# Entry of the SSD stage in a fused attention, SSD and conv-FFN layer: a quarter of the second output row ahead of the first row's second half, z tiles and weight splits in written order, GpSimd's z products and ScalarE's clamps later

## The chip, the core and the metric

The kernel runs on one core of a Trainium2 chip. TensorE (PE) multiplies matrices out of SBUF into PSUM, which has eight banks. VectorE (DVE), ScalarE (ACT) and GpSimd (POOL) work on tiles of 128 partitions; SyncE (SP) issues most DMAs. Each engine takes its own instructions strictly in order and waits at semaphores for the others. The metric is the device time of one execution in microseconds (us), smaller is better. Before the change it is 1199.05 us, the median of 3 runs from 1198.35 to 1201.15.

## What is computed

One layer on 1024 rows of 1024 columns: a norm with modulation, one input projection, attention beside a Mamba-2 scan (SSD), the output projection with a gated residual, a second norm and a convolutional feed-forward net. The change lies in the SSD part and in the output projection:

```python
z, xbc, dt_raw, q, k, v = jnp.split(h @ w_in[l], IN_SPLITS, axis=-1)
...
y = ssd_scan(xs * dt[..., None], dt * A, bm, cm)
y = y + d_skip.astype(jnp.float32)[:, None] * xs
y = y.reshape(b, s, SSD_WIDTH) * jax.nn.silu(z.astype(jnp.float32))
return rmsnorm(y, norm_w).astype(z.dtype)
...
x = x + g_m * (jnp.concatenate([y_ssd, y_att], axis=-1) @ w_out[l])
```

## The kernel before

Every large product is made of three matmuls: each operand is split into a high part, which ScalarE rounds, and a low part, which VectorE gets by subtraction, and TensorE adds high by high, high by low and low by high (`split`, line 84, and `mm3`, line 79). So each operand of a product costs one ScalarE and one VectorE instruction before TensorE may use it.

The 1024 rows are worked in 8 blocks of 128 rows (NT = 8). In the order of the program:

1. The norm, the projection and the attention (to about 300 us) fill `ya`, the attention half of the mixer's output, block by block.
2. The convolved columns fill `xs`, `bt_` and `ct_`. Then come **z tiles** (`z_tile`, line 765): 8 tiles of one half of the z columns (`ch` 1, with dt), then 8 tiles of the other half (`ch` 0), each 24 matmuls into a PSUM tile named `zps` or `s`, a Tanh or Silu on ScalarE and a product on VectorE into `zs`. Behind the first tile of `ch` 0 stands `dt_prep`, which makes the decays (`sm`, `ex3`, `acc_`) for all chunks, and `ssd_pre` for chunk 0.
3. During the same tiles the output projection's weights are split (`wout_split`, line 731) into the room that the z tiles' left operand gives up: slots 0 to 3 (`hH0`, `hL0`), the weights of the attention part, and behind chunk 0 the slots 4 to 7 (`hH1`, `hL1`), those of the SSD part, in 8 pieces of 512 columns scaled by the norm's weight.
4. **The SSD loop** (from line 1061) goes over chunks c = 0 to 7 of 128 rows. `ssd_y` multiplies the masked decay matrices with the inputs (`ydp`, 8 small matmuls), the state with C (`yop`) and B with the inputs (`stp`), and adds them up on VectorE. `ssd_norm` multiplies by z and normalizes: VectorE, ScalarE's Square, two GpSimd instructions for the inverse root (`rstd`), ScalarE's scale. `ssd_turn` transposes the result into `xs`. `ssd_pre` prepares the next chunk: `xdt` on VectorE, `xdd` on GpSimd, 8 clamps (Relu) of the decay rows `cr` on ScalarE, four matmuls into `xps`, `cb` on VectorE, two Exp on ScalarE into `th` and two products of `th` and `cb` on VectorE, which `ydp` of the next chunk needs.
5. Between these, `wout_half(n)` fills TensorE: 24 matmuls of the output projection for block n // 2, the attention part for even n, the SSD part for odd n. They go to two PSUM banks (`wops`), one for each half of the output columns, and the two parts of a block add up in them. The left operand is `yhl`, split from `ya` or `xs` by `wout_rhs`; the odd halves need `xs` after `ssd_turn`. `wout_row` then adds the residual and takes the second norm.

Before the change chunk c goes with half n = c. The halves 8 to 15 follow in the next stage, between the transposes of the second norm (`h_raw`).

The Tile framework places instructions by a scheduler, not always as written: within an engine the order is free as far as data allow, unless `tc.issue_after(i)` puts an instruction behind `i` on the same engine, or `InOrder` (line 49) is switched on. The SSD loop's matmuls are chained in written order by `pe`; the z tiles' are not. GpSimd's product of the finished z with the decay (`zs` times `sm["t"]`, line 867) stands at the end of `ssd_pre` and is free to go early: 6 of the 8 stand ahead of all other GpSimd work of the stage.

Of the kernel before, what the change touches and what calls it, by code (L numbers as in the profile page):

```python
# [68 lines left out]
def tile_block(ctx: ExitStack, tc: tile.TileContext, x, ccol, pk, w_ada, w_first, w_ft, w_z,  # L69
# [41 lines left out]
    def stat(n=1):  # L111
# [3 lines left out]
        stc[0] += n  # L115
        return a

    def rstd(ms, eps=EPS):
        n = ms.shape[-1]
        r = stat(n)  # L120
        G.tensor_scalar(ms, ms, eps, 1.0, op0=ALU.add, op1=ALU.mult)
        G.tensor_tensor(r, ms, mhalf[:, 0:n], ALU.pow)
        return r

    nc.sync.dma_start(cc, ccol)
# [605 lines left out]
    def wout_split(slot, t):  # L731
        dh, j = WORDER[slot]
        h, l = (n[slot // 4][:, slot % 4].rearrange("p a b -> p (a b)") for n in (hth, htl))
        with tc.issue_after(pin[0]), tc.issue_after(pin[1]):
            if j < 2:
                split(h, l, t, A, V)
            else:
                for b in range(2):
                    c = slice(512 * b, 512 * b + 512)
                    k = SNW + order[2 * j + b]  # L740
                    split(h[:, c], l[:, c], t[:, c], A, V, scale=pkt[:, k:k + 1])
# [23 lines left out]
    def z_tile(ch, st, wz):  # L765
        if st < 2 or st // 2 == (3, 2)[ch]:
            ps = psv.tile([P, 512], F32, tag=("acc", "pv")[st % 2], bufs=1, name="zps")[:, 0:260]
        else:
            ps = s_tile()[:, 0:260]
        for kt in range(KT):  # L770
            mm3(ps, hth[st // 4][:, st % 4, kt, :], htl[st // 4][:, st % 4, kt, :],
                wz[kt // 2][0][:, kt % 2, :],
                wz[kt // 2][1][:, kt % 2, :], kt == 0, kt == KT - 1)
        if ch == 1:
            A.activation(zs[:, st, 260:512], ps[:, 0:252], AF.Silu)
            V.tensor_tensor(zs[:, st, 512:520], ps[:, 252:260], pkt[:, DTB:DTB + 8], ALU.add)
            return
        z = zs[:, st, 0:260]
        A.activation(z, ps[:, 0:260], AF.Tanh)
        zlast[:] = [V.scalar_tensor_tensor(z, z, 1.0, ps[:, 0:260], op0=ALU.add, op1=ALU.mult).ins]  # L780

    def dt_prep():
        dtr = zs[:, :, 512:520]
# [45 lines left out]
    def pe(op, *a, **k):  # L829
        with tc.issue_after(chain[0]) if chain and chain[0] else ExitStack():  # L830
            i = op(*a, **k)  # L831
        if chain:
            chain[0] = i.ins

    def ssd_pre(c, xp_, between=None):
# [3 lines left out]
        V.tensor_tensor(h8(xdt), h8(xs[:, c, :]), hb("dt", c), ALU.mult)  # L839
        G.tensor_tensor(h8(xdd), h8(xdt), hb("de", c), ALU.mult)  # L840
        ms_ = []
        cr = bcp.tile([P, 8, P], F32, tag="rm", bufs=2, name="cr")
        nc.sync.dma_start(cr, rows_from(acd, 8 * c, 8))
        for g in range(2):
            for k in range(4 * g, 4 * g + 4):
                a = acc_[:, 8 * c + k:8 * c + k + 1]
                A.activation(cr[:, k], cr[:, k], AF.Relu, scale=-1.0, bias=a)
# [15 lines left out]
            pin2 = V.tensor_tensor(m, m, cb[:, g:g + 1, :].to_broadcast([P, 4, P]), ALU.mult)  # L863
            ms_.append(m)
        pin[:] = [pin1.ins, pin2.ins]
        with tc.issue_after(pin1.ins):
            G.tensor_tensor(h8(zs[:, c, 0:512]), h8(zs[:, c, 0:512]), hb("t", c), ALU.mult)
        return xdt, xdd, cb, ms_

    wz = wz_weights(1)  # L870
# [22 lines left out]
    wz = wz_weights(0)  # L893
    wout_get(3, 6)
    for st in range(NT):
        z_tile(0, st, wz)
        if st == 0:
            dt_prep()
            pin0 = list(pin)
            pre0 = ssd_pre(0, tp_tile)  # L900
            pin[:] = pin0
# [21 lines left out]
        return ps2b.tile([P, 512], F32, tag="x", bufs=PB[1], name="xps")  # L923

    def ssd_tile(name):
        return ps2a.tile([P, 512], F32, tag="ssd", bufs=PB[3], name=name)

    def ssd_y(c, xdt, xdd, cb, ms_):
        cs = slice(c * P, (c + 1) * P)
# [13 lines left out]
        if c < NT - 1:  # L943
            stp = ssd_tile("stp")
            for g in range(2):
                pe(T.matmul, stp[:, g * 256:g * 256 + 256], cb[:, 2 + g, :],
                   xdd[:, g * 256:g * 256 + 256], start=True, stop=True)
            if c > 0:
                G.tensor_tensor(h8(cur), h8(prev), hb("cd", c), ALU.mult)
# [6 lines left out]
            V.tensor_tensor(y, y, t, ALU.add)  # L956
        return y, t

    gated = []

    def ssd_norm(c, y, t, at=None):
        with tc.issue_after(at) if at else ExitStack():
            gated[:] = [V.tensor_tensor(y, y, zs[:, c, 0:512], ALU.mult).ins]
        ms = stat()
        A.activation(t, y, AF.Square, accum_out=ms)
        r = rstd(ms, 512.0 * EPS)
        A.activation(y, y, AF.Copy, scale=r)

    def ssd_turn(c, y):
        tps = x_tile()  # L970
        for j in range(4):
            pe(T.transpose, tps[:, j * P:(j + 1) * P], y[:, j * P:(j + 1) * P], ident)
        A.activation(xs[:, c, :], tps, AF.Copy)


    x1d = dram.tile([S, D], F32, name="x1d")
# [21 lines left out]
    def wout_half(n, ks=slice(0, 8), fill=()):  # L998
        st, part = n // 2, n % 2
        if ks.start == 0:  # L1000
            if part == 0:
                if not xrs:
                    xrs.append(wu.tile([P, 2, 2, 512], F32, tag="w2", bufs=1, name="xr"))
                xr_[st] = xrs[0][:, st % 2]
                nc.sync.dma_start(xr_[st].rearrange("p a b -> p (a b)"), x[st * P:(st + 1) * P, :])
                wps[st] = [ps2b.tile([P, 512], F32, tag="wo", bufs=PB[0], name="wops")
                           for _ in range(2)]
            for q in ((0,), (2,))[n] if n < 2 else (n + 1,):
# [52 lines left out]
    for c in range(NT):  # L1061
# [4 lines left out]
            ssd_turn(*turn)  # L1066
        if c == 1:
            at = wout_rhs(0, 1)
        if c > 1:
            ssd_norm(c, y, t)  # L1070
        turn = (c, y)
        if c < NT - 1:
            pre = ssd_pre(c + 1, x_tile, lambda: wout_half(c, slice(0, 3)))
            if c < 2:
                ssd_norm(c, y, t, at)
            row_scale(pin[0])
            wout_half(c, slice(3, 8))
            if c == 0:
                for j in range(4, 8):
                    pin[:] = zlast + gated  # L1080
                    wout_split(j, wt[j])
        else:
            wout_half(c)
    ssd_turn(*turn)
    chain[:] = []
    row_scale()
# [605 lines left out]
```

## Time and profile before

| quantity | value |
|---|---|
| median of 3 runs | 1199.05 us |
| the profiled execution, whole | 1199.13 us |
| its span, first to last instruction | 1197.4 us |
| TensorE busy | 1166.5 us (97%), mean granted clock 0.990 |
| VectorE, ScalarE, GpSimd busy | 909.2, 588.5, 157.4 us |
| last z tile's last matmul ends | 408.77 us |
| first `ydp` of the SSD loop starts | 413.56 us |
| `ydp` of chunk 2 starts | 439.23 us |
| end of the 16 output halves | about 549.2 us |

A row of the timeline reads: start, duration, engine, line, operation, output<-inputs, size, and in brackets how long the engine was idle before it and what released it. A row with xN merges N instructions in a row. In a table of stretches, each engine has its busy time and number of instructions; PEclk is the clock granted to TensorE as a share of full speed. Engine busy times do not say which wait ends last; the waits and the chain of work do.

### The profile page before, as it was taken

To read this page: it belongs to the slowest core of one execution; us is meant where nothing else is said; L and a number is where in the kernel's file an instruction comes from. 1 tells how busy PE (TensorE), PEld (TensorE's weight loads), DVE (VectorE), ACT (ScalarE), POOL (GpSimd) and SP (SyncE) were. 2 spreads that over 40 slices of the span, in tenths; PEclk is the share of its full clock that TensorE was granted. 3 is DMA by queue.
4 is the path that set the end of the run, shared out by engine and by line. 5 is a ranking of instruction groups with operands and counts; after the bars stand their busy time and mean duration, and the time that the engine had idled before them with its cause. 6 is when DMAs were issued, how large, how long until landed. Compare 5 with 4: busy or idle time off the path is not lost.

```text
span 1197.4 us, 15744 instructions
## 1 busy us (share of the span) xinstructions
PE 1166.5 (97%) x5839; PEld 979.5 (82%) x5839; DVE 909.2 (76%) x1357; ACT 588.5 (49%) x970; POOL 157.4 (13%) x178
## 2 busy tenths in 40 slices
PE   8999999899999899999999999999999999999996
PEld 7778888788789888888788888888888888888885
DVE  7736556665795788558999988898888869666986
ACT  5626555564234766577543453344433444433454
POOL 1103343330000545100000000000000000000522
PEclk9999999899999899999999999999999999999998
DMA  9736334201585322240233222332233378633444
GB/s 355 257 91 158 100 125 115 69 1 36 212 273 184 109 86 72 76 145 28 90 130 129 82 88 97 132 109 85 97 106 114 114 260 301 248 116 122 158 133 148
DMA packets 61293, 160.24 MB, mean 134 GB/s; under 512 B 6608, under 2 KB 7072, under 8 KB 59808
## 3 DMA queue, kind: packets, MB, share of 16 engines
q1 hardware_dynamic: 53872, 134.19, 34.1%
q10 hardware_dynamic: 7344, 25.04, 5.3%
q8 instruction: 46, 0.75, 0.3%
q14 instruction: 31, 0.25, 0.1%
HBM read 121.15 MB, written 28.61 MB: 125 GB/s over the span
## 4 chain that ended last, share of the span: by engine, by line
PE 82%; DVE 10%; issue 3%; ACT 2%; DMA 1%; POOL 1%; POOLq 0%; DVEq 0%; ACTq 0%; SPq 0%
PE wops L831 6%; PE dn L82 5%; PE dn L80 5%; PE dn L81 5%; PE uY L80 5%; PE uY L82 5%; PE uY L81 5%; PE uX L82 3%; PE uX L80 3%; PE uZ L81 3%; PE uZ L80 3%; PE uX L81 3%; PE uZ L82 3%; PE s L80 2%; PE s L81 2%
## 5 line engine op out<-in xcount | busy, mean ns | idle before, releaser
L81 PE MATMUL dn<-w 128*128 128x512 f32 x296 | 108.1, 391 | 0.0
L80 PE MATMUL dn<-w 128*128 128x512 f32 x296 | 108.1, 391 | 0.0
L82 PE MATMUL dn<-w 128*128 128x512 f32 x296 | 100.2, 391 | 0.2 <-DVE w L90 0.2
L80 PE MATMUL uY<-tH,w 128*128 128x512 f32 x248 | 97.2, 392 | 0.0
L81 PE MATMUL uY<-tL,w 128*128 128x512 f32 x248 | 97.0, 391 | 0.0
L82 PE MATMUL uY<-tH,w 128*128 128x512 f32 x248 | 96.9, 391 | 0.0
L1553 POOL TENSOR_TENSOR ya<-ya,xs 128x512 f32<-128x512 f32 x4 | 17.2, 4334 | 557.7 <-ACT xs L1549 557.7
L89 ACT ACTIVATE w<-ya 128x1024 fp32r<-128x1024 f32 (+1 forms) x41 | 39.2, 956 | 87.3 <-PE uY L82 84.2
L831 PE MATMUL wops<-hH,yhl 128*128 128x512 f32 x224 | 72.7, 397 | 0.0
L82 PEld LDWEIGHTS dn<-w 128*128 128x128 f32 x296 | 55.4, 188 | 13.2 <-DVE w L90 1.1
L80 PEld LDWEIGHTS dn<-w 128*128 128x128 f32 x296 | 55.5, 188 | 12.4
L81 PEld LDWEIGHTS dn<-w 128*128 128x128 f32 x296 | 55.6, 188 | 12.2
L529 POOL TENSOR_SCALAR p<-p,st 128x640 f32<-128x640 f32 (+4 forms) x64 | 49.1, 775 | 111.3 <-DVE st L528 108.2
L523 DVE CUSTOM_DVE_ANT_0 p<-s,bias 128x640 f32<-128x640 f32 (+4 forms) x58 | 38.4, 675 | 25.7 <-PE tp L558 9.4
L89 ACT ACTIVATE w<-xs 128x1024 fp32r<-128x1024 f32 (+1 forms) x41 | 39.1, 954 | 37.3 <-PE uY L82 33.3
L90 DVE TENSOR_TENSOR pt<-tp,pt 128x512 fp32r<-128x512 f32 (+2 forms) x72 | 41.9, 596 | 17.9 <-ACT pt L89 17.5
L82 PEld LDWEIGHTS uY<-tH,w 128*128 128x128 f32 x248 | 46.5, 188 | 10.5
L80 PEld LDWEIGHTS uY<-tH,w 128*128 128x128 f32 x248 | 46.5, 188 | 10.3
L81 PEld LDWEIGHTS uY<-tL,w 128*128 128x128 f32 x248 | 46.6, 188 | 10.2
L80 PE MATMUL s<-hH,wh 128*128 128x512 f32 x128 | 50.6, 395 | 1.2 <-DVE ct L640 1.2
L1227 DVE SCALAR_TENSOR_TENSOR a<-cv,pkt,a 128x1023 f32<-128x1023 f32 (+1 forms) x40 | 51.0, 1278 | 0.1
L526 ACT ACTIVATE p<-p,st 128x640 f32<-128x640 f32 (+4 forms) x64 | 44.0, 690 | 13.6 <-DVE st L523 13.0
(494 smaller groups left out, 3408.4 us busy)
## 6 DMA issues: line engine op xcount, KB each, us to landing
wos<-in_w_ada_dram SPq DMA_DIRECT2D x24, 512.0 KB, 4.4
gz<-a ACTq DMA_DIRECT2D x10, 1024.0 KB, 4.9
ya<-in_w_up_dram SPq DMA_DIRECT2D x11, 768.0 KB, 4.1
xs<-in_w_up_dram SPq DMA_DIRECT2D x11, 768.0 KB, 4.2
adat<-in_w_ada_dram SPq DMA_DIRECT2D x16, 512.0 KB, 6.2
raws<-in_w_ft_dram SPq DMA_DIRECT2D x14, 512.0 KB, 3.6
qk<-qk SPq DMA_DIRECT2D x56, 128.0 KB, 2.3
gy<-a ACTq DMA_DIRECT2D x10, 512.0 KB, 2.6
```

Source lines behind the costliest of these rows:

```text
L80: T.matmul(ps, lh, rh, start=start, stop=False, skip_group_check=more)
L81: T.matmul(ps, lh, rl, start=False, stop=False, skip_group_check=more)
L82: T.matmul(ps, ll, rh, start=False, stop=stop, skip_group_check=more)
L89: i = A.activation(hi, src, AF.Copy) if ehi is A else ehi.tensor_copy(hi, src)
L90: return i, elo.tensor_tensor(lo, src, f32(hi), ALU.subtract)
L523: V.tensor_tensor_reduce(out=dst, in0=src, in1=bsl, scale=-1.0, scalar=3e38, op0=ALU.add, op1=ALU.min, accum_out=nm)
L526: A.activation(pv_, pv_, AF.Exp, scale=-1.0, bias=nm, accum_out=rs)
L529: last_g.append(G.tensor_scalar(pv_, pv_, rr, 1.0, op0=ALU.mult, op1=ALU.mult).ins)
L831: i = op(*a, **k)
L1227: V.scalar_tensor_tensor(a[:, j:S], c[:, 0:S - j], w[2 - j], a[:, j:S], op0=ALU.mult, op1=ALU.add)
L1553: G.tensor_tensor(src, src, fnr[:, halves[1]], ALU.mult)
```

## The change

- **Row 1 early.** In the SSD loop the halves no longer go with the chunk one by one. Chunk 0 has half 0, chunk 1 has the first 12 matmuls of half 2 (attention part of block 1, first output half) and then half 1, chunk 2 the other 12 of half 2 and half 3, chunk c from 3 on half c + 1. Half 8 so moves from the next stage into chunk 7. The early quarter has a PSUM bank of its own (tag `w1`); in exchange `ydp`, `yop` and `stp` share 3 banks in place of 4. The left operand of half 2 is split beside that of half 0.
- **z tiles in order.** TensorE's z tiles 4 to 7 of `ch` 0 are issued in written order; before, tile 5 came last. Weight slots 0 to 3 are split one each behind z tiles 2 to 5. Slots 4 to 7 are pinned: ScalarE's part behind the last tile's Tanh (slot 4) or behind chunk 0's norm (slots 5 to 7), VectorE's part behind chunk 1's `th` products.
- **GpSimd.** The z products go one by one: for chunks 0 and 1 behind the skip product `yy`, for later chunks behind their own `xdd`. For chunk 1, `xdd`, `yy` and the state product stand behind chunk 0's inverse root.
- **ScalarE.** The clamps of a chunk go behind the Exp of the chunk before (chunks 1 and 2) or behind the turn of chunk 0 (from chunk 2 on); the Exp of chunk 1 go behind chunk 0's Square.

The rows that follow are the programs' instructions in issue order (line, operation, output<-inputs, size; numbers tell buffers apart).

GpSimd from the first z product of the second half of the z columns to the state product of chunk 2, before:

```order
L867 TENSOR_TENSOR zs_2916<-zs_2916,sm_t_2918 128x512 x6
L936 TENSOR_TENSOR yy_4131<-xs_2902,sm_p_2920 128x512
L936 TENSOR_TENSOR yy_4234<-xs_2902,sm_p_2920 128x512
L840 TENSOR_TENSOR xdd_3859<-xdt_3858,ex3_2923 128x512
L840 TENSOR_TENSOR xdd_4140<-xdt_4139,ex3_2923 128x512
L867 TENSOR_TENSOR zs_2916<-zs_2916,sm_t_2918 128x512 x2
L840 TENSOR_TENSOR xdd_4252<-xdt_4251,ex3_2923 128x512
L949 TENSOR_TENSOR state0_4098<-state1_4099,ex3_2923 128x512
L121 TENSOR_SCALAR st1_72<-st1_72 128x1
L122 TENSOR_TENSOR st1_72<-st1_72,mhalf_70 128x1
```

and now, from chunk 0's inverse root (the two `st1` rows) on:

```order
L123 TENSOR_SCALAR st1_72<-st1_72 128x1
L124 TENSOR_TENSOR st1_72<-st1_72,mhalf_70 128x1
L857 TENSOR_TENSOR xdd_4145<-xdt_4144,ex3_2923 128x512
L960 TENSOR_TENSOR yy_4236<-xs_2902,sm_p_2920 128x512
L848 TENSOR_TENSOR zs_2916<-zs_2916,sm_t_2918 128x512
L976 TENSOR_TENSOR state0_4097<-state1_4098,ex3_2923 128x512
L857 TENSOR_TENSOR xdd_4255<-xdt_4254,ex3_2923 128x512
L848 TENSOR_TENSOR zs_2916<-zs_2916,sm_t_2918 128x512
L960 TENSOR_TENSOR yy_4343<-xs_2902,sm_p_2920 128x512
L857 TENSOR_TENSOR xdd_4385<-xdt_4384,ex3_2923 128x512
L848 TENSOR_TENSOR zs_2916<-zs_2916,sm_t_2918 128x512
L976 TENSOR_TENSOR state1_4098<-state0_4097,ex3_2923 128x512
```

Six of the eight z products stood ahead of all else and the other two ahead of chunk 2's `xdd`. Now each stands in its own chunk: the piece behind chunk 0's inverse root holds ten products, three of them z products.

VectorE in chunk 1, from the weight pieces (`hL1`) to the low part of chunk 0's turned result (`yhl`<-`xs`), before:

```order
L87 SCALAR_TENSOR_TENSOR hL1_87<-wos_2926,pkt_66,hH1_85 128x512 x4
L87 SCALAR_TENSOR_TENSOR hL1_87<-raws_68,pkt_66,hH1_85 128x512 x2
L87 SCALAR_TENSOR_TENSOR hL1_87<-wos_2926,pkt_66,hH1_85 128x512 x2
L856 TENSOR_TENSOR cb_4154<-xps_4149,tle1_2924 128x512
L863 TENSOR_TENSOR th_4172<-th_4172,cb_4154 128x512
L863 TENSOR_TENSOR th_4179<-th_4179,cb_4154 128x512
L90 TENSOR_TENSOR yhl_4248<-xs_2902,yhl_4248 128x512
```

and now:

```order
L884 TENSOR_TENSOR th_4186<-th_4186,cb_4159 128x512
L746 SCALAR_TENSOR_TENSOR hL1_87<-wos_2926,pkt_66,hH1_85 128x512 x4
L746 SCALAR_TENSOR_TENSOR hL1_87<-raws_68,pkt_66,hH1_85 128x512 x2
L746 SCALAR_TENSOR_TENSOR hL1_87<-wos_2926,pkt_66,hH1_85 128x512 x2
L980 TENSOR_TENSOR yy_4236<-ydp_4227,yy_4236 128x512
L855 TENSOR_TENSOR xdt_4384<-xs_2902,sm_dt_2921 128x512
L982 TENSOR_TENSOR yt_4239<-yop_4240,ex3_2923 128x512
L977 TENSOR_TENSOR state0_4097<-stp_4243,state0_4097 128x512
L876 TENSOR_TENSOR cb_4269<-xps_4264,tle1_2924 128x512
L983 TENSOR_TENSOR yy_4236<-yy_4236,yt_4239 128x512
L90 TENSOR_TENSOR yhl_4251<-xs_2902,yhl_4251 128x512
```

The weight pieces moved behind the two `th` products, and the low part moved behind six instructions of chunk 1's own sums.

TensorE in chunk 1, from the state's product on, now; the first `wops_4169` row opens the SSD part of block 0 (half 1), the rows of `wops_4272` are the early quarter of block 1:

```order
L838 MATMUL yop_4240<-state1_4098,ct1_2909 128x256
L838 MATMUL stp_4243<-xdd_4145,cb_4159 128x256 x2
L838 MATMUL xps_4264<-ct0_2908,bt0_2906 128x128
L838 MATMUL xps_4264<-ct1_2909,bt1_2907 128x128
L838 MATMUL xps_4264<-ident_69,bt0_2906 128x128
L838 MATMUL xps_4264<-ident_69,bt1_2907 128x128
L838 MATMUL wops_4272<-hH0_84,yhl_4166 128x512
...
L838 MATMUL wops_4169<-hH1_85,yhl_4251 128x512
L838 MATMUL wops_4169<-hL1_87,yhl_4251 128x512
L838 MATMUL wops_4169<-hH1_85,yhl_4251 128x512 x2
```

Before, the half 1 stood right behind the `xps` rows.

The diff, cut to its core:

```diff
@@ rstd
+        powd[:] = [G.tensor_tensor(r, ms, mhalf[:, 0:n], ALU.pow).ins]
@@ wout_split
-        with tc.issue_after(pin[0]), tc.issue_after(pin[1]):
-            if j < 2:
-                split(h, l, t, A, V)
...
+            with tc.issue_after(pin[0]):
+                A.activation(h[:, c], t[:, c], AF.Copy, scale=sc)
+            with tc.issue_after(pin[1]):
+                if j < 2:
+                    V.tensor_tensor(l[:, c], t[:, c], f32(h[:, c]), ALU.subtract)
...
+    def z_fine(c, at):
+        with tc.issue_after(at):
+            zfine[:] = [G.tensor_tensor(h8(zs[:, c, 0:512]), h8(zs[:, c, 0:512]), hb("t", c),
+                                        ALU.mult).ins]
@@ ssd_pre
-        G.tensor_tensor(h8(xdd), h8(xdt), hb("de", c), ALU.mult)
+        with tc.issue_after(powd[0]) if c == 1 else ExitStack():
+            xddi = G.tensor_tensor(h8(xdd), h8(xdt), hb("de", c), ALU.mult)
...
-                A.activation(cr[:, k], cr[:, k], AF.Relu, scale=-1.0, bias=a)
+                with ExitStack() as es:
+                    for i in expd + (turned[0:1] if c > 1 else []):
+                        es.enter_context(tc.issue_after(i))
+                    A.activation(cr[:, k], cr[:, k], AF.Relu, scale=-1.0, bias=a)
...
-            pin1 = A.activation(m, cr[:, 4 * g:4 * g + 4], AF.Exp, scale=-1.0)
+            with tc.issue_after(gated[2]) if c == 1 else ExitStack():
+                pin1 = A.activation(m, cr[:, 4 * g:4 * g + 4], AF.Exp, scale=-1.0)
...
-        with tc.issue_after(pin1.ins):
-            G.tensor_tensor(h8(zs[:, c, 0:512]), h8(zs[:, c, 0:512]), hb("t", c), ALU.mult)
+        expd[:] = [pin1.ins] if c < 2 else []
+        if c > 1:
+            z_fine(c, xddi.ins)
@@ z tiles of ch 0
+        if st == 4:
+            T.on, T.last = True, None
         z_tile(0, st, wz)
...
-        if st == 3:
-            for j in (0, 1, 2):
-                wout_split(j, wt[j])
-            wout_get(7)
-            wout_split(3, wt[3])
+        if 2 <= st < 6:
+            pin[:] = zlast
+            wout_split(st - 2, wt[st - 2])
+            if st == 4:
+                wout_get(7)
@@ ssd_tile
-        return ps2a.tile([P, 512], F32, tag="ssd", bufs=PB[3], name=name)
+        return ps2a.tile([P, 512], F32, tag="ssd", bufs=3, name=name)
@@ ssd_y
-        G.tensor_tensor(h8(y), h8(xs[:, c, :]), hb("p", c), ALU.mult)
+        with tc.issue_after(powd[0]) if c == 1 else ExitStack():
+            i = G.tensor_tensor(h8(y), h8(xs[:, c, :]), hb("p", c), ALU.mult)
+        if c < 2:
+            z_fine(c, i.ins)
@@ wout_half
+            if len(wps[st]) <= dh:
+                wps[st].append(ps2a.tile([P, 512], F32, tag="w1", bufs=1, name="wops") if n == 2 and not dh else
+                               ps2b.tile([P, 512], F32, tag="wo", bufs=PB[0], name="wops"))
@@ SSD loop
+        if c == 2:
+            wout_half(2, slice(4, 8))
+            wout_rhs(1, 1)
...
+        n, k = ((0, slice(0, 3)), (2, slice(0, 4)), (3, slice(0, 3)))[c] if c < 3 else (c + 1, slice(0, 3))
         if c < NT - 1:
+            if c == 0:
+                ssd_norm(c, y, t)
-            pre = ssd_pre(c + 1, x_tile, lambda: wout_half(c, slice(0, 3)))
+            pre = ssd_pre(c + 1, x_tile, lambda: wout_half(n, k))
+            late = pin[1]
...
-                    pin[:] = zlast + gated
+                    pin[:] = (zlast if j == 4 else gated)[0], late
@@ next stage
-        for n in (0, 1):
-            wout_half(8 + sts[0] + n)
+        for n in (9,) if sts[0] == 0 else (10, 11):
+            wout_half(n)
```

More of the change, by code (lines that the diff above doesn't have):

```diff
@@ L116, in stat @@
         return a
+    powd = []
     def rstd(ms, eps=EPS):
@@ L733, in wout_split @@
         h, l = (n[slot // 4][:, slot % 4].rearrange("p a b -> p (a b)") for n in (hth, htl))
-        with tc.issue_after(pin[0]), tc.issue_after(pin[1]):
-            if j < 2:
-                split(h, l, t, A, V)
[L737 to L741, printed above, removed]
+        for b in range(1 if j < 2 else 2):
+            c = slice(0, 1024) if j < 2 else slice(512 * b, 512 * b + 512)
+            k = SNW + order[2 * j + b]
+            sc = 1.0 if j < 2 else pkt[:, k:k + 1]
+            with tc.issue_after(pin[0]):
[3 more added lines that the diff above has]
+                    V.tensor_tensor(l[:, c], t[:, c], f32(h[:, c]), ALU.subtract)
+                else:
+                    V.scalar_tensor_tensor(l[:, c], t[:, c], sc, f32(h[:, c]), op0=ALU.mult,
+                                           op1=ALU.subtract)
         ws[dh] += [(h[:, k:k + 512], l[:, k:k + 512]) for k in (0, 512)]
@@ L778, in z_tile @@
         z = zs[:, st, 0:260]
-        A.activation(z, ps[:, 0:260], AF.Tanh)
-        zlast[:] = [V.scalar_tensor_tensor(z, z, 1.0, ps[:, 0:260], op0=ALU.add, op1=ALU.mult).ins]
+        i = A.activation(z, ps[:, 0:260], AF.Tanh)
+        zlast[:] = [i.ins, V.scalar_tensor_tensor(z, z, 1.0, ps[:, 0:260], op0=ALU.add,
+                                                  op1=ALU.mult).ins]
     def dt_prep():
@@ L948, in ssd_y @@
             if c > 0:
-                G.tensor_tensor(h8(cur), h8(prev), hb("cd", c), ALU.mult)
+                with tc.issue_after(powd[0]) if c == 1 else ExitStack():
+                    G.tensor_tensor(h8(cur), h8(prev), hb("cd", c), ALU.mult)
                 V.tensor_tensor(cur, stp, cur, ALU.add)
@@ L957, in ssd_y @@
         return y, t
-    gated = []
     def ssd_norm(c, y, t, at=None):
         with tc.issue_after(at) if at else ExitStack():
-            gated[:] = [V.tensor_tensor(y, y, zs[:, c, 0:512], ALU.mult).ins]
+            i = V.tensor_tensor(y, y, zs[:, c, 0:512], ALU.mult)
         ms = stat()
-        A.activation(t, y, AF.Square, accum_out=ms)
+        j = A.activation(t, y, AF.Square, accum_out=ms)
         r = rstd(ms, 512.0 * EPS)
-        A.activation(y, y, AF.Copy, scale=r)
+        gated[:] = [A.activation(y, y, AF.Copy, scale=r).ins, i.ins, j.ins]
     def ssd_turn(c, y):
@@ L972, in ssd_turn @@
             pe(T.transpose, tps[:, j * P:(j + 1) * P], y[:, j * P:(j + 1) * P], ident)
[L973 removed]
+        turned.append(A.activation(xs[:, c, :], tps, AF.Copy).ins)
     x1d = dram.tile([S, D], F32, name="x1d")
@@ L1005, in wout_half @@
                 nc.sync.dma_start(xr_[st].rearrange("p a b -> p (a b)"), x[st * P:(st + 1) * P, :])
-                wps[st] = [ps2b.tile([P, 512], F32, tag="wo", bufs=PB[0], name="wops")
-                           for _ in range(2)]
-            for q in ((0,), (2,))[n] if n < 2 else (n + 1,):
+                wps[st] = []
+            for q in {0: (0, 2), 1: (), 2: ()}.get(n, (n + 1,)):
                 wout_rhs(q // 2, q % 2)
```

15 lines of the change are left out of this document (9 added, 6 removed).

## The prediction

> **What bounds the kernel now.** The page comes first: TensorE is busy nearly all the time, so a change pays only where TensorE waits or runs at a lower clock.
>
> ```profile
> PE 1166.5 (97%) x5839; PEld 979.5 (82%) x5839; DVE 909.2 (76%) x1357; ACT 588.5 (49%) x970; POOL 157.4 (13%) x178
> ```
>
> Then the table of stretches around the change (first number behind the comma: TensorE's busy time; PEclk stands ahead of the DMA share):
>
> ```profile
> 405.00:410.00 5.00, 3.77 (x32) 3.56 (x30) 5.00 (x8) 5.00 (x15) 2.70 (x4) 1.00 0.08 28
> 410.00:415.00 5.00, 1.44 (x7) 1.44 (x7) 3.50 (x5) 5.00 (x14) 5.00 (x5) 0.79 0.28 105
> 415.00:420.00 5.00, 5.00 (x22) 4.64 (x22) 2.65 (x4) 2.44 (x5) 3.60 (x4) 0.53 0.19 54
> 425.00:430.00 5.00, 3.21 (x25) 2.81 (x24) 4.01 (x7) 2.52 (x5) 1.04 (x1) 1.00 0.00 0
> 430.00:435.00 5.00, 5.00 (x20) 4.14 (x19) 4.06 (x7) 1.60 (x5) 1.84 (x2) 0.66 0.27 105
> 440.00:540.00 100.00, 100.00 (x542) 85.69 (x541) 67.31 (x95) 65.82 (x138) 26.26 (x31) 1.00 0.30 102
> ```
>
> TensorE loses 1.23 + 3.56 + 1.79 = 6.6 us of work in two holes, and its clock falls behind each. From 440 to 540 nothing is lost. What ended the two waits:
>
> ```profile
> PE ydp L831 <- DVE zs L780: 4.8, 1, 4.8
> PE ydp L831 <- DVE th L863: 1.8, 1, 1.8
> ```
>
> Both are VectorE: the evacuation of the last z tile, and a `th` product. The clock in single microseconds (the number behind the count):
>
> ```profile
> 413.00:414.00 1.00, 0.44 (x2) 0.50 0.00 0
> 419.00:420.00 1.00, 1.00 (x8) 0.64 0.78 246
> 430.00:431.00 1.00, 1.00 (x4) 0.50 0.00 0
> 433.00:434.00 1.00, 1.00 (x8) 0.81 0.09 33
> ```
>
> It is half from 413 to about 419.6 and again from 430 to about 433.4. The places to reckon from, and one chunk at full speed:
>
> ```profile
> 408.49 0.28 PE L82 MATMUL s<-wzh,hL 128*128 128x260 f32 x1
> 413.56 3.68 PE L831 MATMUL ydp<-xdt,th 128*128 128x64 f32 x16 [4.79 <-DVE zs L780]
> 439.23 1.89 PE L831 MATMUL ydp<-xdt,th 128*128 128x64 f32 x16
> 440.96 1.08 PE L831 MATMUL yop<-state,ct 128*128 128x256 f32 x4
> 441.88 1.03 PE L831 MATMUL stp<-xdd,cb 128*128 128x256 f32 x4
> 442.74 0.60 PE L831 MATMUL xps<-ident,yy 128*128 128x128 f32 x4
> 443.18 0.61 PE L831 MATMUL xps<-ct,bt 128*128 128x128 f32 x4
> 444.01 5.49 PE wops L831 x24
> 449.34 1.89 PE L831 MATMUL ydp<-xdt,th 128*128 128x64 f32 x16
> ```
>
> From the starts: `ydp` 1.73, `yop` 0.92, `stp` 0.86, the turn 0.44, 24 `wops` 5.49 (0.229 each), and `xps` 449.34 - 443.18 - 5.49 = 0.67.
>
> **Step 1, the entry.** In today's program tile 5 of the z tiles comes last, its evacuation ended at 413.5, and `ydp` takes its bank. In order, tile 5 ends some 6 us earlier, and tile 7, now last, has a bank that `ydp` doesn't take. What then decides is the second `th` product, behind the third and fourth weight pieces (`hL0`):
>
> ```profile
> 398.27 1.22 DVE L90 TENSOR_TENSOR hL<-wst,hH 128x1024 fp32r<-128x1024 f32 x1
> 402.53 2.06 DVE L90 TENSOR_TENSOR hL<-raws,hH 128x1024 fp32r<-128x1024 f32 x1
> 408.98 1.41 DVE L863 TENSOR_TENSOR th<-th,cb 128x512 f32<-128x512 f32 x1
> ```
>
> The piece takes 1.22 alone and 2.06 while GpSimd makes z products; those are gone from this stretch, except for three products from 405.4 on. Following VectorE's new order with these durations I get the second `th` product at about 409.45. TensorE ends its z tiles at 408.77 as before and spends 0.87 on the first half of `ydp`, so it waits at most 0.1. Without the hole the clock stays up. Then chunk 0 costs 0.1 + 1.73 + 0.86 + 0.67 + 5.49 + 0.44 = 9.29, and `ydp` to `xps` of chunk 1 cost 1.73 + 0.92 + 0.86 + 0.67 = 4.18: 408.77 + 13.47 = 422.2. The early quarter of block 1 (12 x 0.229 = 2.75) lies behind it, its operand ready since 405: 425.0.
>
> **Step 2, the wait that comes instead.** Half 1 follows. Its third matmul (425.0 + 0.46 = 425.4) reads `yhl`'s low part, which VectorE now makes behind two `th` products, eight weight pieces and six sums of chunk 1. What GpSimd does to these:
>
> ```profile
> 419.15 1.57 DVE L87 SCALAR_TENSOR_TENSOR hL<-wos,pkt,hH 128x512 fp32r<-128x512 f32 x1
> 420.65 1.53 DVE L87 SCALAR_TENSOR_TENSOR hL<-wos,pkt,hH 128x512 fp32r<-128x512 f32 x1
> 423.42 0.74 DVE L87 SCALAR_TENSOR_TENSOR hL<-raws,pkt,hH 128x512 fp32r<-128x512 f32 x1
> 415.70 1.04 POOL L867 TENSOR_TENSOR zs<-zs,sm_t 128x512 f32<-128x512 f32 x1
> 420.13 1.49 POOL L949 TENSOR_TENSOR state<-state,ex 128x512 f32<-128x512 f32 x1
> 430.46 0.68 DVE L839 TENSOR_TENSOR xdt<-xs,sm_dt 128x512 f32<-128x512 f32 x1
> 431.06 0.68 DVE L90 TENSOR_TENSOR yhl<-ya,yhl 128x512 fp32r<-128x512 f32 x1
> ```
>
> Side by side, a VectorE piece and a GpSimd product of 512 columns take turns, one pair in about 1.47; alone the piece takes 0.66 from start to start, other VectorE instructions 0.60. Instructions that read PSUM keep their 0.68 beside GpSimd. GpSimd's row now waits for chunk 0's inverse root, and seven products stand behind it:
>
> ```profile
> 438.41 0.19 POOL L121 TENSOR_SCALAR st<-st 128x1 f32<-128x1 f32 x1 [3.20 <-ACT yt L965]
> 439.27 0.72 ACT L967 ACTIVATE yy<-yy,st 128x512 f32<-128x512 f32 x1
> ```
>
> With chunk 0's `ydp` done at 410.5, three sums, Square, and root end near 414.2 (root: 0.86 by these rows). The first `th` product ends at 414.4. From there seven pairs (second `th` product and six pieces against seven GpSimd products): 414.4 + 7 x 1.47 = 424.7; two pieces alone 1.3: 426.0; six sums 3.6, of which the last waits 0.3 for a z product: 429.8; then the low part waits for the state product (1.0) and takes 0.55: **431.4**. TensorE waits 431.4 - 425.4 = 6.0 us, on `yhl`. ScalarE isn't late: six weight pieces and 13 clamps put `yhl`'s high part near 423.6 by these rows (0.61 and 0.30 each):
>
> ```profile
> 410.71 1.95 ACT L86 ACTIVATE hH<-wos,pkt 128x512 fp32r<-128x512 f32 x3
> 421.77 2.45 ACT L847 ACTIVATE cr<-cr,acc 128x128 f32<-128x128 f32 x8 [1.48 <-DMA cr<-acd]
> ```
>
> After the 4.79 us hole the clock was half for about 6.1 us, after the 1.79 us one for 3.4 us. So 3.4 to 6.8 us at half clock follow this one: a loss of 1.7 to 3.4, I take the middle, 2.55. The other 22 matmuls cost 22 x 0.229 = 5.04. `ydp` of chunk 2 starts at 431.4 + 5.04 + 2.55 = 439.0, against 439.23, with 12 more matmuls done (2.75): **gain 3.0 us**.
>
> [...]
>
> **Step 3, the rest.** One z product per chunk from chunk 2 to 6 lies where GpSimd was idle for some 4 us a chunk; VectorE loses up to 0.85 in each. In the chunk with the least room:
>
> ```profile
> 448.07 1.28 DVE L863 TENSOR_TENSOR th<-th,cb 128x512 f32<-128x512 f32 x2
> ```
>
> the first product ends at 448.7 against the need at 449.34, the second at 449.35 against 450.2: 0.6 to 0.85 of room. So 0 to 0.25 in each of five chunks; I take 0.3 in all. The clamps' new order costs nothing (they run in ScalarE's idle half, 65.8 of 100 us busy; without that cover 0.3 per clamp). Three banks for `ydp`, `yop`, `stp`: each is read within 3 us of being filled and comes round a chunk (10.1) later, 0. Tile 5 in order waits for tile 3's evacuation, which I place 1.7 before the need, 0; queued behind it are two z tiles. SP's loads keep their order up to chunk 2; the one weight load that waits for slot 2's split (about 403) is needed at 417. In the next stage half 8 is missing as a filler; the same transposes and halves remain, TensorE had no hole there, 0 with bounds of -0.5 to +0.5.
>
> **Sum.** 1199.13 (profiled execution, span 1197.4 and 1.73 around it; 0.08 above the median) - 3.0 + 0.3 = **1196.4**. Bounds of the unknown price, the turns: with none, VectorE has the low part at 424.5, nothing waits, `ydp` of chunk 2 starts at 430.4, gain 11.6, 1187.8 with the 0.3. With GpSimd's 1.04 added in full (1.9 later, as above), 1198.3. The clock's bounds alone, 1.7 and 3.4, give 1195.6 to 1197.3; one and a half turns fewer than seven (1.47 - 0.6 = 0.87 each, 1.3) and the lower clock loss give 1194.2. The forecast's own range is 1194.2 to 1198.3.
>
> **Rivals.** *Short wait*: TensorE finds `yhl` early because GpSimd's products meet fewer VectorE instructions than I count. For it: it takes only a shift of GpSimd by some us; against it: both queues are back to back there. With half of the delay the low part comes at 428, the wait is 2.6, half clock costs 1.7: gain 7.3, 1192.1; without any, 1187.8. [...]
>
> *The entry keeps its wait*: `ydp`'s bank is freed by the last z tile after all (evacuated near 410.2). Then 1.4 us of hole and 1.7 for the clock shift the `th` chain, and the wait at `yhl` shortens by less than that. I estimate that 1.5 to 3.0 of the gain are lost, so 0 to 1.5 is left: with the 0.3 of step 3 1197.9 to 1199.4, near 1198.5, no measurable change.
>
> *Slower*: the z products make VectorE late in every chunk from 2 to 6. A product that pushes the `th` pair back by its whole turn (1.47) less the room of 0.6 costs 0.9 a chunk, 4.4 in five, and two holes with a clock loss of 1.7 add 3.4: 1196.1 + 7.8 = 1203.9. It decides from 0.6 a chunk on, where it eats the gain. For it: VectorE's 8.5 of 10 us; against it: the three sums that read PSUM leave GpSimd its turns.
>
> **How the numbers follow.** Forecast 0.5 (1194.2 to 1198.3), short wait 0.2 (1187.8 to 1194), entry keeps its wait 0.16 (1197.5 to 1199.5), slower 0.14 (1200 to 1206). A measurement of this kernel tells about 0.2%, 2.4 us, from no change: below 1196.7 lie some 0.6 of the forecast (0.31) and the short wait (0.2), 0.51; above 1201.5 0.13; between them 0.36. For 8 in 10 the range is 1189.5 to 1200.5: it leaves out the far end of the short wait and most of the slower case.
>
> **What would show it.** Right: no wait of `ydp` on `zs`, full clock at 413 to 425, a wait of `wops` on VectorE's `yhl` of 4 to 8 us with half clock behind it, pairs of 1.47 in the `hL` pieces. Wrong: `wops` after `xps` without a wait (short wait), `ydp` of chunk 0 waiting over 1 us (entry), or waits of `ydp` on `th` in chunks 3 to 7 (slower).

## The result and the profile after

The changed kernel takes 1198.5 us (median of 14 runs, 1197.07 to 1201.51) against 1198.7 us of the kernel before (14 runs, 1195.91 to 1201.15): a ratio of 1.0003, 95% interval 0.9994 to 1.0013 (estimated from all runs, so not the quotient of the two medians). The change makes no difference that can be measured. The forecast was 1196.4, 2.7 us less than the execution that it was reckoned from, inside a range of 1189.5 to 1200.5. The measured time lies in that range, but just outside the narrower 1194.2 to 1198.3 that the prediction gave its own mechanism.

The entry looks as the prediction drew it. The stretches of the profile after (columns as in the prediction):

```profile
405.00:410.00 5.00, 5.00 (x44) 5.00 (x44) 3.74 (x6) 5.00 (x14) 1.42 (x1) 1.00 0.40 124
410.00:415.00 5.00, 5.00 (x37) 4.64 (x36) 3.40 (x7) 4.01 (x11) 2.04 (x2) 1.00 0.26 93
415.00:420.00 5.00, 5.00 (x28) 4.22 (x27) 4.51 (x4) 5.00 (x9) 4.89 (x6) 1.00 0.35 105
425.00:430.00 5.00, 2.08 (x10) 1.37 (x8) 5.00 (x8) 2.02 (x6) 1.76 (x2) 1.00 0.27 105
430.00:435.00 5.00, 1.88 (x5) 1.49 (x6) 4.87 (x7) 0.72 (x2) 2.87 (x4) 0.67 0.01 2
435.00:440.00 5.00, 5.00 (x16) 3.97 (x15) 0.69 (x1) 1.83 (x5) 0.56 (x1) 0.65 0.14 52
```

From 405 to 420 TensorE is full and at full clock: both the hole and its half clock are gone. From 425 to 435 it loses 2.92 + 3.12 = 6.0 us of work in one hole, and behind it the clock is half for a while. The waits of TensorE that are new:

```profile
PE wops L838 <- DVE yhl L90: 6.6, 2, 6.0
PE xps L62 <- ACT ya L62: 0.7, 1, 0.7
PE ydp L838 <- DVE th L884: 0.2, 1, 0.2
```

The places on TensorE's timeline (start, duration, in brackets the wait ahead of it): the last z matmul, `ydp` of chunk 0, the third matmul of half 1, `ydp` of chunk 2, half 3, `ydp` of chunk 4, and the transposes of the last row in the next stage.

```profile
410.16 0.29 PE L62 MATMUL zps<-wzh,hL 128*128 128x260 f32 x1
410.29 1.90 PE L838 MATMUL ydp<-xdt,th 128*128 128x64 f32 x16
433.12 1.22 PE L838 MATMUL wops<-hH,yhl 128*128 128x512 f32 x2 [6.04 <-DVE yhl L90]
440.77 1.89 PE L838 MATMUL ydp<-xdt,th 128*128 128x64 f32 x16
449.35 0.74 PE L838 MATMUL wops<-hH,yhl 128*128 128x512 f32 x2 [0.59 <-DVE yhl L90]
464.99 1.97 PE L838 MATMUL ydp<-xdt,th 128*128 128x64 f32 x16 [0.25 <-DVE th L884]
555.74 0.66 PE L62 MATMUL xps<-ident,ya 128*128 128x128 f32 x4 [0.69 <-ACT ya L62]
```

The same transposes before the change, without a wait:

```profile
554.62 0.60 PE L62 MATMUL xps<-ident,ya 128*128 128x128 f32 x4
```

What VectorE did before and during TensorE's wait (427.08 to 433.12):

```profile
417.56 5.87 DVE L746 SCALAR_TENSOR_TENSOR hL<-wos,pkt,hH 128x512 fp32r<-128x512 f32 x4
423.35 2.98 DVE L746 SCALAR_TENSOR_TENSOR hL<-raws,pkt,hH 128x512 fp32r<-128x512 f32 x2
426.26 1.40 DVE L746 SCALAR_TENSOR_TENSOR hL<-wos,pkt,hH 128x512 fp32r<-128x512 f32 x2
427.58 0.68 DVE L980 TENSOR_TENSOR yy<-ydp,yy 128x512 f32<-128x512 f32 x1
430.58 1.04 DVE L983 TENSOR_TENSOR yy<-yy,yt 128x512 f32<-128x512 f32 x1
431.54 1.52 DVE L90 TENSOR_TENSOR yhl<-xs,yhl 128x512 fp32r<-128x512 f32 x1
```

and GpSimd beside it:

```profile
415.82 1.26 POOL L857 TENSOR_TENSOR xdd<-xdt,ex 128x512 f32<-128x512 f32 x1
424.30 1.49 POOL L960 TENSOR_TENSOR yy<-xs,sm_p 128x512 f32<-128x512 f32 x1
431.03 1.49 POOL L976 TENSOR_TENSOR state<-state,ex 128x512 f32<-128x512 f32 x1
```

These rows show the turns: while GpSimd's seven products run (415.82 to 425.8), four pieces take 423.35 - 417.56 = 5.79, 1.45 each; the last two, with GpSimd idle, take 0.66 each. Then come the sums. The low part could have been made from 425.1 on, when ScalarE's high part was there, but it ends at 433.06.

**Where the gain went.** The profiled executions are 1198.6 and 1197.4 us in span, so this one is 1.2 longer, though the entry was passed as forecast. Three pieces add up to that. The last z matmul starts at 410.16 in place of 408.49: 1.67 later, and of what the change touches only the order of the z tiles and of the splits beside them lies ahead of it. From there to the last row's transposes it is 145.58 in place of 146.13, 0.55 less. Behind them it is 642.86 and 642.78. The 1.67 are the clock's: both kernels wait near 47 us for the same instructions (1.51, 0.17 and 0.40 us within some 3 us), and then the clock stays up in one and falls in the other. The same microseconds before the change and after it:

```profile
49.00:50.00 1.00, 1.00 (x12) 1.00 (x10) 0.00 (x0) 1.00 (x3) 0.00 (x0) 1.00 0.96 393
```

```profile
49.00:50.00 1.00, 1.00 (x7) 1.00 (x8) 0.00 (x0) 1.00 (x3) 0.00 (x0) 0.72 0.93 344
52.00:53.00 1.00, 1.00 (x4) 0.80 (x4) 0.40 (x2) 0.77 (x2) 0.55 (x1) 0.58 0.00 0
```

By these rows the clock is half from 49.44 to 52.84, and 3.4 us at half clock cost 1.7. Of the nine profiled executions shown here three have this spell (after, e3, e5), six have not. Near 230, still far ahead of the change, the same happens on a larger scale: TensorE waits 2.15 us in all nine, and the half clock behind it lasts 6.8 us in six, 3.4 in two (e5, e6) and is absent in one (e1). So two spans differ by some 2 us and more for no reason in the change, and the span of e1's profile is short partly for this reason. In what follows the stage alone is compared: from the start of the last z matmul.

### The profile page after: what moved, and what is told of

It reads as the page before. It is cut to its first block, busy times and chain, and to the rows that moved or that the text cites. A ratio compares the mean times of both kernels' runs of the same rounds, so it can differ in the third digit from the quotient of the medians.

```text
span 1198.6 us, 15751 instructions
## 1 busy us (share of the span) xinstructions
PE 1165.8 (97%) x5839; PEld 978.5 (82%) x5839; DVE 910.6 (76%) x1357; ACT 587.2 (49%) x970; POOL 159.8 (13%) x178
## 4 chain that ended last, share of the span: by engine, by line
PE 79%; DVE 12%; issue 4%; ACT 3%; DMA 1%; POOL 1%; SPq 0%; POOLq 0%; DVEq 0%; ACTq 0%
PE dn L82 5%; PE dn L80 5%; PE dn L81 5%; PE wops L838 5%; PE uY L82 5%; PE uY L80 5%; PE uY L81 5%; PE uX L82 3%; PE uX L80 3%; PE uZ L81 3%; PE uX L81 3%; PE uZ L80 3%; PE uZ L82 3%; PE s L80 2%; PE s L81 2%
## 5 line engine op out<-in xcount | busy, mean ns | idle before, releaser
L838 PEld LDWEIGHTS wops<-hH,yhl 128*128 128x128 f32 x224 | 43.1, 194 | 16.1 <-DVE yhl L90 7.5
L81 PEld LDWEIGHTS uY<-tL,w 128*128 128x128 f32 x248 | 46.6, 188 | 10.2
```

What stands on the lines that cost most here:

```text
L81: T.matmul(ps, lh, rl, start=False, stop=False, skip_group_check=more)
```

## The experiments

Theory A says that VectorE's order sets the wait: the low part stands behind work that isn't urgent. B says that GpSimd's turns make it. C says that VectorE simply has too much to do between the z tiles and chunk 2, in any order. Each ratio is against runs of the kernel before that were taken beside it: their medians are 1198.06 for e1 to e4 and 1198.88 for e5 to e7.

| kernel | median us | ratio to before, 95% | last z matmul to `ydp` of chunk 2 | to the last row's transposes |
|---|---|---|---|---|
| before | 1198.7 | 1 | 30.74 (12 `wops` fewer) | 146.13 |
| after | 1198.5 | 1.0003 [0.9994, 1.0013] | 30.61 | 145.58 |
| e1 low part first | 1192.11 | 0.9952 [0.9936, 0.9968] | 23.27 | 138.35 |
| e2 no z products | 1196.13 | 0.9981 [0.9971, 0.9991] | 27.45 | 142.20 |
| e3 quarter late | 1199.6 | 1.0015 [1.0003, 1.0027] | 30.40 (12 fewer) | 147.25 |
| e4 low part after four pieces | 1193.83 | 0.9966 [0.9953, 0.998] | 22.22 | 140.71 |
| e5 the same, chunk 1's low part too | 1191.58 | 0.9941 [0.9925, 0.9958] | 22.23 | 138.11 |
| e6 z products early | 1197.66 | 0.9994 [0.9983, 1.0005] | 30.49 | 145.25 |
| e7 before, z tiles in order | 1202.21 | 1.0025 [1.0012, 1.0038] | holes lie among the z tiles | not comparable |

**e1, low part first.** One place undone in the order of VectorE:

```diff
@@ SSD loop, against the changed kernel
         if c == 1:
             ssd_turn(*turn)
+            low[:] = [at := wout_rhs(0, 1)]
+            V.after = at
         y, t = ssd_y(c, *pre)
+        V.after = None
         if c > 1:
             ssd_turn(*turn)
-        if c == 1:
-            at = wout_rhs(0, 1)
...
```

`V.after` puts VectorE's instructions behind `at`; elsewhere in this kernel it also holds `cb` and the next `xdt` behind the low part, and the residual of block 0 behind chunk 1's gate.

> The change, with one thing undone: VectorE makes the low part of chunk 0's turned result ahead of chunk 1's sums, right behind the eight weight pieces, as it stood ahead of the sums in the program before. Theory A (VectorE's order: the low part waits behind work that is not urgent): the low part ends near 428.2 on the scale of the changed kernel's profile, in which the z tiles end at 410.4; TensorE waits about 1.2 us there in place of 6.0, and ydp of chunk 2 starts some 6.5 us earlier, 23.5 to 24.5 us behind the z tiles' end in place of 30.3; with or without a spell of half clock (1.7) the time falls by 5 to 7, to about 1192. Theory B (the turns with GpSimd's products make the wait, wherever the low part stands): only the low part's own turn (0.8) and the turn of the sum ahead of it (0.4) are saved, some 1.2 us. Theory C (VectorE has too much work between the z tiles and chunk 2 in any order): the wait goes from half 1 to the th products of chunk 2, ydp of chunk 2 starts no more than 2 to 3 us earlier, about 1196.

```profile
406.15 0.28 PE L67 MATMUL zps<-wzh,hL 128*128 128x260 f32 x1
424.30 0.73 PE L843 MATMUL wops<-hH,yhl 128*128 128x512 f32 x2 [1.23 <-DVE yhl L95]
429.42 1.89 PE L843 MATMUL ydp<-xdt,th 128*128 128x64 f32 x16
```

The wait is 1.23, as A has it, `ydp` of chunk 2 comes 23.3 behind the z tiles (23.5 to 24.5 was expected), and no half clock follows. The median is 5.9 below its own runs of before (1198.06), and the stage is 7.2 shorter than the changed kernel's. B would have saved 1.2, C 2 to 3: neither is the whole. VectorE's work is the same; only its order changed.

**e2, no z products.** GpSimd's eight products of `zs` and `sm_t` are left out, so the gate lacks that factor:

```diff
     def z_fine(c, at):
-        with tc.issue_after(at):
-            zfine[:] = [G.tensor_tensor(...)]
+        return
```

> The change without GpSimd's eight z products (the gate's factor is left out of the computation), nothing else. Theory A: two products among the eight weight pieces (0.87 each) and one beside the last sums and the low part (about 1) are gone; the wait at the low part shrinks from 6.0 to about 3.3, and the short waits of later chunks (0.56, 0.25) go too; time 3 to 4 us less, about 1195. Theory B: the wait goes nearly whole, 5 us or more and the clock's loss behind it, about 1190. Theory C: as A at the low part, but the th products of chunk 2 take up most of it, about 1197.

```profile
407.91 0.28 PE L62 MATMUL zps<-wzh,hL 128*128 128x260 f32 x1
428.62 0.73 PE L838 MATMUL wops<-hH,yhl 128*128 128x512 f32 x2 [3.79 <-DVE yhl L90]
435.36 1.89 PE L838 MATMUL ydp<-xdt,th 128*128 128x64 f32 x16
444.33 0.73 PE L838 MATMUL wops<-hH,yhl 128*128 128x512 f32 x2 [0.98 <-DVE yhl L90]
```

Without the z products the wait is 2.25 shorter (3.3 left was expected, 3.8 measured). So the turns are a real part, but order, with 4.8 in e1, is the larger one. The stage is 3.4 shorter than the changed kernel's, as A has it; the median is 1.1 above A's 1195. Against what A expected, the short wait of half 3 didn't go: it grew to 0.98. It isn't made by the z products. The wait of `ydp` of chunk 4 did go.

**e3, the quarter late.**

```diff
-            wout_half(2, slice(4, 8))
+            wout_half(2)
...
-        n, k = ((0, slice(0, 3)), (2, slice(0, 4)), (3, slice(0, 3)))[c] if c < 3 else ...
+        n, k = ((0, slice(0, 3)), (1, slice(0, 3)), (3, slice(0, 3)))[c] if c < 3 else ...
...
-            if c == 1:
-                wout_half(1)
-            else:
-                wout_half(n, slice(3, 8))
+            wout_half(n, slice(3, 8))
```

> The change without the early quarter: the first 12 matmuls of half 2 stand in chunk 2 with the other 12, half 1 stands right behind chunk 1's xps. VectorE's and GpSimd's orders are those of the change. Theory A: TensorE comes to the low part 2.75 us earlier and waits 8.8 in place of 6.0; ydp of chunk 2 starts where it did, and chunk 2 is 2.75 longer: 1201.2. A rival (the quarter fills time that a later hole gives back anyway): no difference, 1198.5.

```profile
425.16 0.50 PE L838 MATMUL wops<-hH,yhl 128*128 128x512 f32 x1 [1.28 <-ACT yhl L89]
433.13 1.22 PE L838 MATMUL wops<-hH,yhl 128*128 128x512 f32 x2 [7.23 <-DVE yhl L90]
456.13 1.89 PE L838 MATMUL ydp<-xdt,th 128*128 128x64 f32 x16
```

TensorE waits 1.28 for the high part, which stands behind ScalarE's clamps, and 7.23 for the low part: 8.5 in all, where 8.8 was expected. But the stage is only 1.67 longer, not 2.75: half 3, now behind all 24 matmuls of half 2, has no wait of 0.59 any more, `ydp` of chunk 2 comes 0.2 earlier, and some 0.3 in chunk 2 aren't traced. So the rival has a share: a later hole gives back 1.1 of the 2.75, and the median, 1199.6, lies between the two expectations. The early quarter is worth some 1.7 us of the stage.

**e4, the low part behind four pieces.** The second half of the weight pieces is issued behind the low part, ScalarE's clamps behind the high part, `xdt` and `xdd` of chunk 3 later, and 3 `wops` of half 2 ahead of the turn of chunk 1:

```diff
         if c == 1:
             ssd_turn(*turn)
+            hi, at = wout_rhs(0, 1)
+            high[:] = [hi]
+            for j in (6, 7):
+                pin[:] = gated[0], at
+                wout_split(j, wt[j])
+            V.on, V.last = True, at2[0]
         y, t = ssd_y(c, *pre)
+        if c == 2:
+            wout_half(2, slice(4, 5))
...
```

> A new order of chunk 1, everything else as changed. VectorE makes the low part behind four of the eight weight pieces (the first column half's), ScalarE its high part ahead of the clamps; then the other four pieces, the state, the sums, the th products, the gate; xdt and xdd of chunk 3 go behind them, and TensorE puts the turn of chunk 1 behind 3 matmuls of half 2. Theory A: the low part ends near 425 against a need at 427, no wait at half 1, no spell of half clock; ydp of chunk 2 starts near 432 to 433 on the changed kernel's scale in place of 440.8, and the time falls by 7 to 9, to about 1190. Theory B: the pieces take their turns all the same, the low part comes near 425 too, but the last pieces stop the second column half; ydp near 435, 1193. Theory C: TensorE waits 3 us or more at the th products of chunk 2, with half clock behind, and the gain is 3 or less, 1195.5 or more.

```profile
430.16 1.97 PE L840 MATMUL ydp<-xdt,th 128*128 128x64 f32 x16 [0.33 <-DVE th L62]
440.79 1.22 PE L840 MATMUL wops<-hH,yhl 128*128 128x512 f32 x2 [2.55 <-DVE yhl L90]
```

Half 1 doesn't wait any more, and `ydp` of chunk 2 comes 22.2 behind the z tiles, as A has it. The 7 to 9 us didn't come, though (4.2 against its own runs of before): TensorE, now earlier, waits 2.55 at the next low part, that of chunk 1, and runs at half clock for 3.4 us behind it. None of the three theories had named that place; that the time is near B's 1193 is luck, since the second column half that B names doesn't wait. VectorE's row says why: ahead of it stand block 0's residual, chunk 2's sums and its gate, and beside it a GpSimd product.

```profile
439.21 1.52 DVE L90 TENSOR_TENSOR yhl<-xs,yhl 128x512 fp32r<-128x512 f32 x1
```

**e5, that low part earlier as well.** Against e4:

```diff
-            V.tensor_tensor(y, y, t, ALU.add)
+            if c != 2:
+                V.tensor_tensor(y, y, t, ALU.add)
...
-            wout_rhs(1, 1)
+            with tc.issue_after(wout_rhs(1, 1)[1]):
+                V.tensor_tensor(y, y, t, ALU.add)
```

> The new order of chunk 1 of the run before (low part behind four weight pieces), and in chunk 2 VectorE makes the low part of chunk 1's turned result ahead of the last sum and the gate of chunk 2. That run removed the wait at half 1, but at half 3 TensorE waited 2.55 for this low part and then ran 3.4 us at half clock (1.7 lost). Theory A (VectorE's order decides, the wait moves to the next low part that is queued too late): the low part of chunk 1 ends near 438.8 on that run's scale in place of 440.7, with a need at 438.2; the wait is 0.6 or less, no half clock, 3.5 to 4.3 less than that run: 1189.5 to 1190.5. Theory C (VectorE has too much to do in any order): the th products of chunk 3, now later, stop ydp of chunk 3 by 1.5 or more, and the gain over that run is 2 or less, 1192 or more.

```profile
431.58 1.97 PE L840 MATMUL ydp<-xdt,th 128*128 128x64 f32 x16 [0.32 <-DVE th L62]
440.30 0.74 PE L840 MATMUL wops<-hH,yhl 128*128 128x512 f32 x2 [0.64 <-DVE yhl L90]
445.86 1.97 PE L840 MATMUL ydp<-xdt,th 128*128 128x64 f32 x16 [0.27 <-DVE th L887]
```

The wait is 0.64, no half clock, and the stage 2.6 shorter than e4's. The median is 1191.58, 7.3 below its own runs of before, where e4 was 4.2 below its own: 3.1 more. The 2.6 and the 3.1 both lie between A's 3.5 and C's 2; against the kernel before the gain is 0.4 to 0.75%. C has a share in it: VectorE is busy without a break from 415 to 456, and `th` is late by some 0.3 in chunks 2, 3 and 4, though not by the 1.5 that C expected. e5 and e1 can't be told apart by the measurement; both beat the kernel before and the changed one.

**e6, z products early.**

```diff
-        if c > 1:
-            z_fine(c, xddi.ins)
+        z_fine(c, pin1.ins)
...
-        if c < 2:
-            z_fine(c, i.ins)
```

> The change, with GpSimd's z products free to go early again, as in the program before (they stand beside the last z tiles; none is left in the chunks). Theory A: two turns fewer among the weight pieces and one fewer beside the sums, as in the run without z products: the wait at chunk 0's low part is near 3.8 in place of 6.0; in exchange the third and fourth weight pieces (hL0) and the th products of chunk 0 take turns with GpSimd, and ydp of chunk 0 waits 0.5 to 1.5: together 1 to 2.5 less than the changed kernel, 1196 to 1197.5. A rival (the late z products are what closed the entry): ydp of chunk 0 waits 3 or more, with half clock behind it, and the time is 1199 or more.

```profile
411.68 1.71 PE L838 MATMUL ydp<-xdt,th 128*128 128x64 f32 x8 [1.98 <-DVE th L884]
432.36 1.15 PE L838 MATMUL wops<-hH,yhl 128*128 128x512 f32 x2 [3.05 <-DVE yhl L90]
```

The wait at the low part falls to 3.05, and the entry gets one of 1.98, on a `th` product: VectorE's instructions ahead of it now take turns (the two `xdt` products together 2.99 in place of 1.29), and so does the product itself (1.52 in place of 0.68). A expected 0.5 to 1.5 here, its rival 3 or more. Each wait is followed by 3.4 us of half clock, so the stage is 0.3 shorter than in the changed kernel where A had 1 to 2.5. Where the z products stand moves the hole; it doesn't fill it.

**e7, the kernel before with z tiles in order.**

```diff
     for st in range(NT):
+        if st == 4:
+            T.on, T.last = True, None
         z_tile(0, st, wz)
...
+    T.on = False
```

> The program before with one part of the change alone: TensorE's z tiles 4 to 7 in written order. Theory A (tile 5 as the last tile is what holds the bank of the first ydp): the hole of 4.8 at the entry closes to 1 or less, and its spell of half clock goes; ydp of chunk 1 still waits for the th products behind the eight weight pieces, 2 to 5 in place of 1.8; ydp of chunk 2 comes 2 to 5 earlier, time 1194 to 1197. A rival (the entry's hole is only passed on, VectorE's weight pieces set chunk 1): ydp of chunk 1 starts where it did, 1198 or more.

```profile
PE ydp L831 <- DVE th L863: 3.6, 1, 3.6
PE s L62 <- DVE zs L780: 2.7, 1, 2.7
...
PE xps L831 <- DVE zs L780: 1.2, 1, 1.2
```

A's time failed: the kernel is slower than before by 0.25%, as only the rival allowed (1198 or more), but `ydp` of chunk 1 doesn't start where it did, as the rival had it: it comes 2.9 later. Two things came as A has them: the wait of the first `ydp` for a bank is gone, and `ydp` of chunk 1 waits 3.6 for `th`. But the four weight splits still stand in a block behind z tile 3, VectorE makes them ahead of the next z tile's evacuation, and now that TensorE may not take the tiles in another order it waits 2.7 in the middle of them, with 6.8 us of half clock behind. That the order before the change, with tile 5 last, was the scheduler's way round this wait fits, and is only argued. In e6, where the z products are as early but the splits are spread one behind each tile, TensorE doesn't wait among the z tiles. So the order of the tiles seems to pay only together with the spread splits; e6 differs from e7 in more than this, so it isn't shown by itself.

## Why the prediction was right, and where a term was not

**Step 1, the entry**, held: `ydp` of chunk 0 starts right behind the last z matmul (410.29), without a wait, at full clock. e7 adds what the step left unsaid: the order of the tiles alone doesn't close the entry's hole, it moves it in among the z tiles. e6 bears out that the z products have to be gone from this stretch: with early ones TensorE waits 1.98.

**Step 2, the wait that comes instead**, held in place and size. The low part was forecast 431.4 - 408.77 = 22.6 behind the z tiles; it ended at 433.06, 22.6 behind their end at 410.45. The marks on the way fit as well: six pieces were done 15.8 behind the z tiles (15.9 forecast), the sums 21.1 (21.0). The wait is 6.04 against 6.0, and the half clock cost (440.77 - 433.12) - 22 x 0.229 = 2.6 against 2.55. The spell itself, from 431.72 to 438.56 by the rows below, is 6.84 long, but its beginning falls into the wait and costs nothing there. The forecast had taken the middle between 1.7 and 3.4 without a reason for it, so that this term fits so well is luck. The clock after the change, in single microseconds:

```profile
431.00:432.00 1.00, 0.00 (x0) 0.00 (x0) 1.00 (x2) 0.00 (x0) 1.00 (x2) 0.86 0.00 0
438.00:439.00 1.00, 1.00 (x5) 0.81 (x4) 0.48 (x1) 0.11 (x1) 0.00 (x0) 0.72 0.00 0
```

So `ydp` of chunk 2 stood 0.13 earlier (30.61 in place of 30.74 behind the last z matmul) with 2.75 us more of work done: 2.9 gained, 3.0 forecast. The upper end of the forecast's own range, 1198.3, adds GpSimd's 1.04 in full to each turn, with the low part 1.9 later; no run shows that term. In its place the row of 5.79 for four pairs says 1.45 a pair, and the low part came where it was forecast.

**Step 3, the rest, was the term of the sum that was mis-sized**: a loss of 0.3 was forecast. Of the 2.9 gained only 0.55 is left at the last row's transposes, so the loss is 2.3. Three things are in it.

First, half 3 now waits 0.59 for chunk 1's low part, and chunk 2 is 0.25 longer beside that. The sum has no term for this. The prediction went through the late z products and the banks there, but not through the due time of that low part: half 3 went with chunk 3 before and goes with chunk 2 now, so the low part is due some 7 us earlier, while VectorE's place for it is the same, behind the sums and the gate. e2 shows that the z products don't make this wait (0.98 without them, and the same 0.25), e5 that the place does.

Second, the z products. From `ydp` of chunk 3 to `ydp` of chunk 7 the kernel before takes 489.77 - 449.34 = 40.43, the changed one 495.50 - 454.47 = 41.03, and e2, without z products, again 40.43. So they cost 0.6, twice the 0.3 that the step took but less than the 1.25 that it allowed in five chunks. Two thirds of it are lost between `ydp` of chunk 3 and of chunk 4 (464.99 - 454.47 = 10.52 in place of 10.11). Before:

```profile
489.77 1.89 PE L831 MATMUL ydp<-xdt,th 128*128 128x64 f32 x16
```

after:

```profile
454.47 1.89 PE L838 MATMUL ydp<-xdt,th 128*128 128x64 f32 x16
495.50 1.89 PE L838 MATMUL ydp<-xdt,th 128*128 128x64 f32 x16
```

e2:

```profile
449.44 1.89 PE L838 MATMUL ydp<-xdt,th 128*128 128x64 f32 x16
489.87 1.89 PE L838 MATMUL ydp<-xdt,th 128*128 128x64 f32 x16
```

Third, the last row's transposes wait 0.69, and 0.2 more is lost on the way to them: from `ydp` of chunk 7 it is 555.74 - 495.50 = 60.24, where the kernel before took 554.62 - 489.77 = 64.85 with half 8 in it, 59.36 without its 5.49. The step had 0 here, with 0.5 at most. Every kernel here with half 8 moved has this wait, and the two that leave it in the next stage (before, e7) don't. That the half was the filler there fits this, but it wasn't tried by itself. The 0.25 and the 0.2 lie in stalls too short for the view of waits, and their cause stays open.

**The rivals.** *Short wait* fell by the pairs of 1.45, which both queues kept up to the last product. *The entry keeps its wait* fell by 410.29. *Slower* had the right engine, but 0.6 in all and not 0.9 in each of five chunks. The result of *the entry keeps its wait*, a time near 1198.5 and no gain that can be measured, came nonetheless, from step 3 and not from the entry. The forecast was right about the mechanism of the entry and of the new wait, and 2 us too low because of step 3. That the time lies inside the range says less than it seems, since the range is 11 us wide and held that rival's result too.

## What to carry to other kernels

A reorder that closes a hole makes the next consumer early: list what that consumer reads, and where its producer stands in its engine's queue, and do so again for the one behind it. When work is moved up by a stage, every operand of it is due a stage earlier, and its producer has to move as well. Here the place of one low part on VectorE was worth 6 us (e1), while all that the change moved gave 0.55 in this stage as long as that place was wrong.

## What the runs showed of the hardware

Every spell of half clock in this stage was one, two or three times 3.4 us long. They were 3.4 us (behind waits of 1.8, 2.0, 2.55, 3.05 and 3.8), 6.8 us (behind 2.7, 3.6, 4.8 and 6.0) or 10.2 us (behind the 8.5 of e3); waits of 0.98 and 1.23 had none. Outside the stage the same waits of about 2 us near 47 had a spell in three executions of nine, and the 2.15 near 230 had one of 6.8 in six, of 3.4 in two and none in one. So in these runs a wait of 2 to 4 us cost its own length and, differently from one execution to the next, nothing, 1.7 or up to 3.4 on top. Why a spell has one of these lengths, or doesn't come, these runs don't show.
